# Input norm on a transposed copy of the input, by halves of the tokens, and group 0's values with 512 moving columns

## The chip, the cores and the metric

The kernel runs on one core of one Trainium2 chip. The metric is the device time of one execution in microseconds (us), from the first to the last instruction with the launch around them. The engines are TensorE (PE; its weight loads are PEld), VectorE (DVE), ScalarE (ACT), GpSimd (POOL) and SyncE (SP), which here only issues DMAs. The granted clock is the share of full speed that TensorE was given: 1.00 is 2.4 GHz, 0.50 is 1.2 GHz.

## The reference

One decoder block on 1024 tokens of width 1024, in float32: an RMS norm, one wide projection, an LRU mixer and a windowed attention mixer side by side, then a feed-forward part. The change concerns the first lines and the values `v` of attention group 0:

```python
def rms_norm(x, g):
    y = x * lax.rsqrt(jnp.mean(x * x, axis=-1, keepdims=True) + 1e-6)
    return y * g

h = rms_norm(x, pre_mix_norm)
proj = h @ w_in                       # (1024, 1024) @ (1024, 8704)
xr, gr, q, k, v, gates = jnp.split(proj, split_at, axis=-1)
v = v.reshape(B, S, 3, 4, 128)        # 3 groups of 4 heads of 128
```

Groups 1 and 2 take their keys and values at a stride of 4 and 16 tokens; group 0 takes them in order.

## The kernel before

**Precision.** Each float32 operand of a large product is split into a high part `hi` (float32r, one copy on ACT or POOL) and a low part `lo` (one subtraction on DVE or POOL). A product is three matmuls, hi hi, hi lo, lo hi, summed in PSUM (`mm3`, L128 to L133). Matmuls of two plain float32 operands are used for attention scores and values.

**The start.** `x` is loaded in 8 blocks of 128 tokens, tokens on the partitions (`load_x`). For a block, `norm_rows` squares and sums it on ACT (L192), works out the rate in five small operations (`rstd_of`, L176 to L185) and multiplies on DVE (L193). `turn` transposes it with 8 PE transposes (L201) and leaves three copies with channels on the partitions: `hth` (hi, L204), `htl` (lo, L205) and `hf` (full, L206), 2 tiles each of 4 x 128 channels by 1024 tokens. Ten matmuls on zeros (L153) run ahead. The main loop has eight turns of this; three of group 0's four `v_chain` steps stand in it (VAT), the fourth behind it.

**Group 0's values.** `v_weights(pr, 0)` loads and splits the weights of one pair of heads, 256 columns. `v_chain(pr, 0, wv, i)` multiplies 256 tokens, in two pieces of 128, by them: 48 matmuls with 256 moving columns, one copy from PSUM (L405), and after each second step a DMA to the DRAM tile `vd`. There are 4 steps for each of 2 pairs, 384 matmuls.

**Groups 2 and 1.** These use a two by two scheme of seven products instead of eight: tokens and channels are halved into blocks b11, b12, b21, b22, and `x_sums` forms t1 = b12 - b11, t2 = b22 - t1, t4 = b21 - t2, t3 = b22 - b12 on POOL (L457), in place in `hf` and in `x2`, and splits t1, t4, t3 at once (ACT L453, DVE L454). It stands in the loop over the second pair's four `v_chain` steps. t2 is split at L572 and L573 into the halves of `hth` and `htl` that held b12. Then `v_start(2)` does the two products that need only blocks of the input (96 matmuls), and `v_quad(2)` the other five: it loads four blocks of weights a21, a22, a11, a12 into `vr`, forms sums of them (`s3` at L551 on POOL, L552 and L553 on DVE, L554 on POOL), splits them and multiplies. `vr` and the other tiles of the pool `vq` lie in the memory of `hf` and `x2`, which is given back first. `decay_rates` is a chain of 14 DVE operations on 128 x 8 elements for the LRU part (L364 to L377).

**Order.** A tile scheduler orders each engine's queue; `issue_after` adds an edge. All loads of `load` go through SP's queue in the order in which the program has them.

## Time and profile before

| | us |
|---|---|
| median of 3 runs (1767.65 to 1770.36) | 1769.05 |
| the profiled execution, its own time | 1767.89 |
| its span, first to last instruction | 1766.0 |

| engine | busy us | share of the span |
|---|---|---|
| PE | 1683.0 | 95% |
| PEld | 1393.4 | 79% |
| DVE | 1154.1 | 65% |
| POOL | 770.6 | 44% |
| ACT | 753.6 | 43% |

The times of instructions count from the start of the span. What is said of sums refers to the profiled execution; the median is 1.16 above it. A time range of a stage is given with the busy time of every engine in it; an idle engine matters only where the next thing that ends the program waits for it.

### The profile page before, as it was taken

Reading aid. Unit: us, or ns where it says so; the run is one execution under the profiler, and the core shown is the slowest. Engines: PE = TensorE matmul, PEld = TensorE weight load, DVE = VectorE, ACT = ScalarE, POOL = GpSimd, SP = SyncE. Lnnn points to the kernel's source line nnn. Section 1 sums busy time; section 2 is a strip of 40 time slices with the busy share of each in tenths; the row PEclk is TensorE's granted clock in tenths of the full one; section 3 lists DMA queues with packets and bytes.
Section 4 is the critical chain, followed back from the end, with each engine's and each line's share of the span. In section 5 each row is a group of like instructions: output and inputs, shape, how many; then the busy total and the mean of one; then the engine's idle time right before and its main releaser. Section 6 shows DMA issues by size and latency. Waiting matters only on the chain.

```text
span 1766.0 us, 22080 instructions
## 1 busy us (share of the span) xinstructions
PE 1683.0 (95%) x7994; PEld 1393.4 (79%) x7994; DVE 1154.1 (65%) x1669; ACT 753.6 (43%) x1244; POOL 770.6 (44%) x698
## 2 busy tenths in 40 slices
PE   7799999999999998989999999799999999999897
PEld 6789888778787786778888887678888888788685
DVE  6667477687889855654343577855555465558958
ACT  6333356655455532365442244522232222354443
POOL 3433444456354554306233303577656656404503
PEclk8899999999999999999999999899999999999999
DMA  4244343334233366485526752133322222474363
GB/s 174 96 153 137 132 141 125 132 131 149 108 136 127 137 197 190 157 298 214 193 96 250 273 204 84 52 111 113 118 103 100 101 90 101 145 273 157 118 209 113
DMA packets 95437, 262.17 MB, mean 148 GB/s; under 512 B 14448, under 2 KB 22672, under 8 KB 93920
## 3 DMA queue, kind: packets, MB, share of 16 engines
q1 hardware_dynamic: 69504, 178.82, 29.7%
...
HBM read 177.52 MB, written 83.10 MB: 148 GB/s over the span
## 4 chain that ended last, share of the span: by engine, by line
PE 73%; DVE 12%; DMA 5%; issue 4%; POOL 3%; ACT 2%; SPq 1%; DVEq 0%; POOLq 0%; ACTq 0%
PE pq L133 14%; PE pq L132 14%; PE pq L131 14%; PE pd L1199 2%; PE py L133 2%; PE pd L1198 2%; PE pd L1200 2%; PE py L132 2%; PE py L131 2%; DMA rsn<-rtd 2%; PE pv L132 2%; PE pv L133 2%; PE pv L131 2%; PE po L883 2%; DVE wlo L97 1%
## 5 line engine op out<-in xcount | busy, mean ns | idle before, releaser
L133 PE MATMUL pq<-hth,wlo 128*128 128x512 f32 x448 | 177.9, 397 | 7.4 <-DVE wlo L97 7.4
L132 PE MATMUL pq<-htl,whi 128*128 128x512 f32 x448 | 179.8, 401 | 0.0
L131 PE MATMUL pq<-hth,whi 128*128 128x512 f32 x448 | 178.6, 399 | 0.0
L277 POOL TENSOR_TENSOR sb<-wraw 128x512 f32<-128x512 f32 x50 | 67.7, 1353 | 164.3 <-DMA wraw<-in_w_fg 89.2
L96 ACT ACTIVATE whi<-sa 128x1024 fp32r<-128x1024 f32 x50 | 52.9, 1059 | 202.1 <-PE pq L132 128.1
L1199 PE MATMUL pd<-fbl,fah 128*128 128x512 f32 x300 | 117.7, 392 | 7.9 <-DVE fbl L97 7.1
L97 DVE TENSOR_TENSOR wlo<-wraw,whi 128x1024 fp32r<-128x1024 f32 x69 | 105.8, 1533 | 23.9 <-ACT whi L96 21.1
L1200 PE MATMUL pd<-fbh,fal 128*128 128x512 f32 x300 | 116.8, 389 | 0.0
L1198 PE MATMUL pd<-fbh,fah 128*128 128x512 f32 x300 | 116.7, 389 | 0.0
L96 ACT ACTIVATE whi<-wraw 128x1024 fp32r<-128x1024 f32 x69 | 72.8, 1055 | 85.5 <-PE pq L132 31.7
L133 PEld LDWEIGHTS pq<-hth,wlo 128*128 128x128 f32 x448 | 85.2, 190 | 29.3 <-DVE wlo L97 8.8
L319 DVE TENSOR_TENSOR uw<-pq,uw 128x512 f32<-128x512 f32 x100 | 68.3, 683 | 54.8 <-PE pq L133 53.6
L131 PEld LDWEIGHTS pq<-hth,whi 128*128 128x128 f32 x448 | 85.1, 190 | 21.3
L132 PEld LDWEIGHTS pq<-htl,whi 128*128 128x128 f32 x448 | 85.2, 190 | 20.1
L97 DVE TENSOR_TENSOR fal<-ar,fah 128x512 fp32r<-128x512 f32 x75 | 66.9, 892 | 38.4 <-ACT fah L96 38.4
L1105 POOL TENSOR_TENSOR fo<-fo,ut 128x512 f32<-128x512 f32 x44 | 60.1, 1368 | 69.3 <-DVE ut L1104 69.3
L97 DVE TENSOR_TENSOR wlo<-sa,whi 128x1024 fp32r<-128x1024 f32 x50 | 69.7, 1395 | 30.0 <-ACT whi L96 29.9
L591 DVE TENSOR_TENSOR fb<-pq,uw 128x512 f32<-128x512 f32 x84 | 67.8, 808 | 28.6 <-PE pq L133 28.1
L132 PE MATMUL pv<-wlo,hth 128*128 128x256 f32 x256 | 76.1, 297 | 7.7 <-DVE wlo L97 7.7
L133 PE MATMUL pv<-whi,htl 128*128 128x256 f32 x256 | 76.1, 297 | 5.3 <-DVE htl L205 4.4
L132 PE MATMUL pq<-t1l,whi 128*128 128x512 f32 x200 | 78.9, 395 | 0.0
L131 PE MATMUL pq<-t1h,whi 128*128 128x512 f32 x200 | 78.9, 394 | 0.0
...
## 6 DMA issues: line engine op xcount, KB each, us to landing
...
qkd<-fb POOLq DMA_DIRECT2D x24, 512.0 KB, 3.4
qk<-qkd SPq DMA_DIRECT2D x24, 512.0 KB, 9.0
wraw<-in_w_fg SPq DMA_DIRECT2D x24, 512.0 KB, 3.3
wraw<-in_w_fu SPq DMA_DIRECT2D x24, 512.0 KB
...
```

The lines of the kernel that those rows point to most:

```text
L96: A.activation(hi, src, AF.Copy)
L97: (le or V).tensor_sub(lo, src, f(hi))
L131: T.matmul(o, lh, rh, start=(first and i == 0), stop=False)
L132: T.matmul(o, lh, rl, start=False, stop=False)
L133: T.matmul(o, ll, rh, start=False, stop=(last and i == n - 1))
L277: G.tensor_add(sb[:, lo_], r1[:, lo_], r1[:, hi_])
L319: V.tensor_add(y, bank, x)
L591: V.tensor_add(o, half_in(bank, g), half_in(add, g))
L1105: G.tensor_mul(g, g, ut)
L1198: T.matmul(o, ah[:, ts], bh, start=(i == 0), stop=False)
L1199: T.matmul(o, ah[:, ts], bl, start=False, stop=False)
L1200: T.matmul(o, al[:, ts], bh, start=False, stop=(i == NP - 1))
```

## The change

The host gives the kernel `xT`, the transposed input, and the weights of group 0 in four blocks of 256 channels by 512 columns (`w_v0`); `w_v` holds only groups 1 and 2 now. The input is loaded straight into `hf`, channels on the partitions, in eight pieces of 2 x 128 channels by 512 tokens. A sum over channels is then a sum over partitions: `sums` multiplies the squares with a column of ones (32 matmuls of one column for each half of the tokens), `rates` works out the four rates of a partition, writes them on the diagonals of four 128 x 128 blocks and multiplies with a matrix of ones, so that `prb` holds each token's rate on all partitions. `normed` multiplies `hf` by the gain and `prb` in place and splits it. `v0_mm` has tokens stationary and 512 weight columns moving. The constants come over ACT's queue. Two more groups of six matmuls on zeros are written (WARM2). The POOL subtractions of `x_sums` are now `x_diffs`, in two calls of 4 x 1024 columns within the second half; the splits of t1, t3 and t4 (`x_split`) are written behind `v_start(2)`, with `decay_rates` ahead of them.

```diff
-    def turn(xn, t, hi, lo, full):
...
-    for t in range(NT):
...
-        turn(xns[t], t, hth, htl, hf)
-        if t in VAT:
-            v_chain(0, 0, wv, VAT.index(t))
...
-    v_chain(0, 0, wv, 3)
+    def w0_split():
+        j = len(W0)
...
+        split(R0[j], hi, lo, he=G)
...
+    def squares(h, j):
+        SQ[h, j] = sp.tile([128, 2, 512], F32, name="sq", bufs=4)
+        A.activation(SQ[h, j], pair(hf, j, h), AF.Square)
+
+    def sums(h):
+        ss = ps("pss")
+        for j in range(4):
+            for k in range(2):
+                for t in range(4):
+                    T.matmul(ss[:, t:t + 1], SQ[h, j][:, k, 128 * t:128 * t + 128], ones[:, 0:1],
+                             start=(j + k + t == 0), stop=(j == 3 and k == 1), skip_group_check=True)
+        return ss[:, 0:4]
+
+    def rates(ss):
+        s = sp.tile([128, 4], F32, name="rs4", bufs=2)
+        last_act[0] = A.activation(s, ss, AF.Sqrt, bias=epsc, scale=1.0 / D)
...
+        for t in range(4):
+            V.tensor_scalar(dg[:, t], ident, e[:, t:t + 1], None, op0=OP.mult)
+        rb = ps("prb")
+        T.matmul(rb, ones, dg.rearrange("p t n -> p (t n)"), start=True, stop=True)
+        return rb
+
+    def normed(h, j, rb):
+        for k in range(2 * j, 2 * j + 2):
+            x = hf[k // 4][:, k % 4, 512 * h:512 * h + 512]
+            V.scalar_tensor_tensor(x, x, gneg[:, k:k + 1], rb, op0=OP.mult, op1=OP.mult)
+        x, hi = pair(hf, j, h), pair(hth, j, h)
+        last_act[0] = A.activation(hi, x, AF.Copy)
+        last_dve[0] = V.tensor_sub(pair(htl, j, h), x, f(hi))
+
+    def v0_mm(bk, h, j):
+        for k in range(2 * j, 2 * j + 2):
+            wh, wl = (t[:, k % 2] for t in W0[j])
+            for t in range(4):
+                c = slice(512 * h + 128 * t, 512 * h + 128 * t + 128)
+                T.matmul(bk[t], hTh[k][:, c], wh, start=(k == 0), stop=False)
+                T.matmul(bk[t], hTh[k][:, c], wl, start=False, stop=False)
+                T.matmul(bk[t], hTl[k][:, c], wh, start=False, stop=(k == KT - 1))
+
+    def v0_out(bk, h):
+        vs = sp.tile([128, 4, 512], F32, name="vs0", bufs=2)
+        for t in range(4):
+            A.activation(vs[:, t, :], bk[t], AF.Copy)
+        for pr in range(2):
+            G.dma_start(v_block(pr, 0, h), vs[:, :, 256 * pr:256 * pr + 256])
+
+    def x_diffs(j):
+        b11, b12, b21, b22 = (pair(hf, 2 * u + j, h) for u in range(2) for h in range(2))
+        x2p = x2[:, 2 * j:2 * j + 2, :]
+        G.tensor_sub(b11, b12, b11)
+        G.tensor_sub(x2p, b22, b11)
+        G.tensor_sub(b21, b21, x2p)
+        G.tensor_sub(b12, b22, b12)
+
+    for j in range(4):
+        x_load(0, j)
+        squares(0, j)
...
+    ss = sums(0)
+    keep_warm(WARM2)
+    rb = rates(ss)
+    keep_warm(WARM2)
+    bk = [ps("pv") for _ in range(4)]
+    for j in range(4):
+        normed(0, j, rb)
+        with tc.issue_after(last_act[0].ins):
+            squares(1, j)
+        if j == 3:
+            ss1 = sums(1)
+        v0_mm(bk, 0, j)
...
+    rb = rates(ss1)
+    normed(1, 0, rb)
+    with tc.issue_after(last_act[0].ins):
+        v0_out(bk, 0)
+    for j in range(1, 4):
+        normed(1, j, rb)
+    bk = [ps("pv") for _ in range(4)]
+    for j in range(4):
+        v0_mm(bk, 1, j)
+        if j in (1, 3):
+            x_diffs(j // 2)
+    v0_out(bk, 1)
...
-    wv = v_weights(1, 0)
-    for i in range(4):
-        v_chain(1, 0, wv, i)
-        x_sums(4 + i, hf, x2[:, :, 128 * i:128 * i + 128], X1, ("t1", "t3", "t4"))
...
     b = v_start(2)
-    for k in range(4):
-        A.activation(X1["t2"][0][:, k, :], x2[:, k, :], AF.Copy)
-        V.tensor_sub(X1["t2"][1][:, k, :], x2[:, k, :], f(X1["t2"][0][:, k, :]))
+    with tc.issue_after(last_act[0].ins), tc.issue_after(last_dve[0].ins):
+        x_split("t2", x2)
+        x_split("t1", hf[0][:, :, LO])
+        x_split("t3", hf[0][:, :, HI])
+        x_split("t4", hf[1][:, :, LO])
```

On PE the program now starts with these rows (`pw` are the matmuls on zeros, `pss` the sums of squares, `prb` the broadcast rates, `pv` group 0):

```order
L156 MATMUL pw<-wz 128x512 x11
L426 MATMUL pss<-ones,sq 128x1 x8
L156 MATMUL pw<-wz 128x512 x6
L426 MATMUL pss<-ones,sq 128x1 x8
L156 MATMUL pw<-wz 128x512 x5
L426 MATMUL pss<-ones,sq 128x1 x16
L444 MATMUL prb<-dg,ones 128x512
L460 MATMUL pv<-whi,hth_110 128x512
```

The matmuls on zeros of both later calls stand among the sums, and none behind them.

On DVE, in the kernel before, these rows stand in the stretch of group 0's second pass (`lv` is the decay chain, t1l to t4l are the low parts of the sums for groups 2 and 1):

```order
L373 SCALAR_TENSOR_TENSOR lv<-lv 128x8 x6
L374 SCALAR_TENSOR_TENSOR lv<-lv 128x8
L375 SCALAR_TENSOR_TENSOR lv<-lv 128x8
L454 TENSOR_TENSOR t1l_617<-hf_111,t1h_616 128x4x128
L376 TENSOR_SCALAR lv<-lv 128x8
L454 TENSOR_TENSOR t4l_621<-hf_112,t4h_620 128x4x128
L377 TENSOR_SCALAR lv<-lv 128x8
L454 TENSOR_TENSOR t3l_619<-hf_111,t3h_618 128x4x128
```

After the change they stand behind t2 and behind the second weight split of `v_start(2)`, directly ahead of `v_quad(2)` (L619 writes its first outputs, L635 and L636 are its sums of weights):

```order
L529 TENSOR_TENSOR htl_112<-x_116,hth_110 128x2x512
L361 SCALAR_TENSOR_TENSOR lv<-lv 128x8
L98 TENSOR_TENSOR wlo<-wraw,whi 128x1024
L361 SCALAR_TENSOR_TENSOR lv<-lv 128x8 x4
L362 SCALAR_TENSOR_TENSOR lv<-lv 128x8
L363 SCALAR_TENSOR_TENSOR lv<-lv 128x8
L529 TENSOR_TENSOR t1l_552<-hf_114,t1h_551 128x1024 x2
L529 TENSOR_TENSOR t3l_554<-hf_114,t3h_553 128x1024 x2
L529 TENSOR_TENSOR t4l_556<-hf_115,t4h_555 128x1024 x2
L619 TENSOR_TENSOR vs<-pv,vp_689 128x512 x2
L635 TENSOR_TENSOR vr<-vr 128x1024
L636 TENSOR_TENSOR vr<-vr 128x1024
```

The six splits have moved from the loop to the end of it, and read whole tiles of `hf` (hf_114 and hf_115 here) in whose memory `vr` lies.

On POOL the eight subtractions now stand between the issue of the first half's outputs and that of the second's (x_116 is `x2`, vs_394 and vs_521 the two halves of the outputs):

```order
L475 TENSOR_TENSOR hf_114<-hf_114 128x2x512 x2
L469 DMA vd<-vs_394 512x1x256 x2
L476 TENSOR_TENSOR x_116<-hf_115,hf_114 128x1024
L478 TENSOR_TENSOR hf_114<-hf_115,hf_114 128x2x512
L477 TENSOR_TENSOR hf_115<-hf_115,x_116 128x2x512
L476 TENSOR_TENSOR x_116<-hf_115,hf_114 128x1024
L478 TENSOR_TENSOR hf_114<-hf_115,hf_114 128x2x512
L477 TENSOR_TENSOR hf_115<-hf_115,x_116 128x2x512
L469 DMA vd<-vs_521 512x1x256 x2
```

Before, they were 16 of half the size, four to each `v_chain` step of the second pass.

## Rows read from the trace of the kernel before

**Rows 1.** The page: the span, PE's busy time, and the chain that ended last by engine.

```profile
span 1766.0 us, 22080 instructions
PE 1683.0 (95%) x7994; PEld 1393.4 (79%) x7994; DVE 1154.1 (65%) x1669; ACT 753.6 (43%) x1244; POOL 770.6 (44%) x698
PE 73%; DVE 12%; DMA 5%; issue 4%; POOL 3%; ACT 2%; SPq 1%; DVEq 0%; POOLq 0%; ACTq 0%
```

**Rows 2.** Busy time of each engine by stage: from and to, the length, then busy us with the count of instructions for each engine, the granted clock, the share of the DMA engines and GB/s.

```profile
0.00:19.80 19.80, 7.75 (x26) 6.17 (x27) 10.80 (x22) 8.05 (x16) 8.16 (x10) 0.73 0.73 280
19.80:100.80 81.00, 69.09 (x530) 68.06 (x528) 53.69 (x86) 39.28 (x75) 27.54 (x21) 0.90 0.29 101
100.80:105.70 4.90, 1.05 (x5) 0.63 (x5) 4.86 (x6) 3.06 (x3) 3.09 (x2) 0.88 0.18 64
```

**Rows 3.** PE in order of time, the start: start us, duration us, engine, line, operation, out<-in, shape, count, and in brackets the idle time before and what ended it.

```profile
2.02 4.19 PE L153 MATMUL pw<-wz 128*128 128x512 f32 x10 [2.02 <-DVE wz L150]
...
19.82 0.56 PE L131 MATMUL pv<-whi,hth 128*128 128x256 f32 x1
...
26.84 1.91 PE L201 MATMUL pT<-cst,xn 128*128 128x128 f32 x16
```

**Rows 4.** PE in order of time, the end of `v_start(2)` and the beginning of `v_quad(2)`, same columns.

```profile
99.77 0.28 PE L133 MATMUL pv<-whi,htl 128*128 128x256 f32 x1
...
100.48 0.28 PE L133 MATMUL pv<-whi,htl 128*128 128x256 f32 x1
102.23 0.51 PE L131 MATMUL pv<-whi,hth 128*128 128x256 f32 x2 [1.47 <-ACT whi L96]
...
105.67 0.58 PE L132 MATMUL pv<-wlo,hth 128*128 128x256 f32 x1 [1.99 <-DVE wlo L97]
```

**Rows 5.** The other engines in order of time ahead of 105.67, same columns.

```profile
98.61 1.21 DVE L552 TENSOR_TENSOR vr<-vr 128x1024 f32<-128x1024 f32 x1
99.86 1.22 DVE L553 TENSOR_TENSOR vr<-vr 128x1024 f32<-128x1024 f32 x1
...
101.60 2.21 DVE L481 CAST ang<-pos_i 128x512 f32<-128x512 int32 x1
...
104.41 2.34 DVE L97 TENSOR_TENSOR wlo<-vr,whi 128x1024 fp32r<-128x1024 f32 x2
...
101.12 2.00 ACT L96 ACTIVATE whi<-vr 128x1024 fp32r<-128x1024 f32 x2 [5.42 <-DVE vr L553]
...
101.17 2.37 POOL L554 TENSOR_TENSOR vr<-vr 128x1024 f32<-128x1024 f32 x1 [7.48 <-DVE vr L553]
```

**Rows 6.** SP's queue in order of time (the row with a start), and the DMA view of 64 to 84 us: issues by destination and source with their count, KB each and the median us from issue to landing.

```profile
70.66 1.75 SPq L107 DMA_DIRECT2D vr<-in_w_v  x4
...
vr<-in_w_v SPq DMA_DIRECT2D x4, 512.0 KB, 6.9
...
vd<-vs POOLq DMA_DIRECT2D x1, 512.0 KB, 2.9
```

**Rows 7.** DVE and POOL in order of time within the subtractions for groups 2 and 1, same columns as rows 3.

```profile
59.85 0.68 DVE L454 TENSOR_TENSOR t1l<-hf,t1h 128x512 fp32r<-128x512 f32 x1
59.86 1.81 POOL L457 TENSOR_TENSOR hf<-hf,hf 128x512 f32<-128x512 f32 x1
60.46 1.25 DVE L376 TENSOR_SCALAR lv<-lv 128x8 f32<-128x8 f32 x1
61.62 0.68 DVE L454 TENSOR_TENSOR t4l<-hf,t4h 128x512 fp32r<-128x512 f32 x1
61.64 1.78 POOL L457 TENSOR_TENSOR hf<-hf,x 128x512 f32<-128x512 f32 x1
62.22 1.23 DVE L377 TENSOR_SCALAR lv<-lv 128x8 f32<-128x8 f32 x1
```

**Rows 8.** PE later in the program: two matmuls of 512 columns, six apart; all rows of L767, a float32 matmul of attention scores (duration ns least, median and longest, first and last start); and two weight loads that stand close together.

```profile
186.45 0.40 PE L131 MATMUL pq<-hth,whi 128*128 128x512 f32 x1
...
187.85 0.40 PE L131 MATMUL pq<-hth,whi 128*128 128x512 f32 x1
...
L767 PEld LDWEIGHTS psc<-qk x104: 186/192/333, 758.0 to 908.2; 128*128 128x128 f32 x104
...
805.45 0.13 PEld L829 LDWEIGHTS ptr<-cst,rwc 8*128 8x128 f32 x1 [0.37 <-DVE st L783]
805.60 0.20 PEld L871 LDWEIGHTS ppt<-cst,pb 128*128 128x128 f32 x2
```

**Rows 9.** The DMA view of 0 to 12 us: GB/s in 40 equal slices of 0.3 us.

```profile
GB/s 0 0 0 0 0 55 259 96 109 205 341 355 410 437 369 382 273 219 369 424 369 424 424 410 335 335 410 396 423 437 437 410 423 437 437 410 423 423 369 410
```

**Rows 10.** Groups of instructions from 0 to 106 us: busy us, mean ns of one, and idle time before.

```profile
L96 ACT ACTIVATE whi<-vr 128x1024 fp32r<-128x1024 f32 x3 | 3.1, 1052 | 5.9 <-DVE vr L553 5.4 <-POOL vr L554 0.4
...
L551 POOL TENSOR_TENSOR vs<-vr 128x1024 f32<-128x1024 f32 x1 | 2.4, 2419 | 0.0
...
L97 DVE TENSOR_TENSOR wlo<-vr,whi 128x1024 fp32r<-128x1024 f32 x2 | 2.3, 1208 | 0.0
...
L536 DVE TENSOR_TENSOR vs<-pv,vp 128x512 f32<-128x512 f32 x2 | 1.4, 688 | 6.7 <-issue 6.7
...
L183 DVE TENSOR_SCALAR rq<-rq 128x1 f32<-128x1 f32 x8 | 1.2, 154 | 0.3
```

**Rows 11.** Busy time by stage, same columns as rows 2, after the idle time before 105.67.

```profile
106.00:108.00 2.00, 2.00 (x11) 2.00 (x11) 2.00 (x3) 0.00 (x0) 0.00 (x0) 0.50 0.78 231
108.00:110.00 2.00, 2.00 (x11) 2.00 (x11) 0.55 (x2) 0.00 (x0) 0.00 (x0) 0.50 0.93 295
110.00:112.00 2.00, 2.00 (x14) 2.00 (x14) 1.02 (x2) 0.00 (x0) 0.00 (x0) 0.66 0.81 291
```

More of the change, by code (lines that the diff above doesn't have):

```diff
@@ L29 @@
 WARM = 10
+WARM2 = 6
 PRE = 4
@@ L148, in block, with keep_warm @@
     A.activation(warm, warm, AF.Sqrt)
-    wz = b4("wz", F32R)
+    epsc = sp.tile([128, 1], F32, name="epsc")
+    V.memset(epsc, EPS)
+    gneg = sp.tile([128, 8], F32, name="gneg")
+    wz = sp.tile([128, 640], F32R, name="wz")
     V.memset(f(wz), 0.0)
+    ones = sp.tile([128, 128], F32, name="ones")
+    V.memset(ones, 1.0)
     pw = ps("pw")
-    for i in range(WARM):
-        T.matmul(pw, wz[:, 0:128], wz[:, 128:640], start=True, stop=True)
-    xs = [load_x(0)]
-    gpre = gain_bc(a["g_pre"], "gpre", A)
+    def keep_warm(n):
+        for i in range(n):
+            T.matmul(pw, wz[:, 0:128], wz[:, 128:640], start=True, stop=True)
+    keep_warm(WARM)
     cst = const.tile([128, C_END], F32, name="cst")
-    c_ld = G.dma_start(cst, a["consts"])
-    vec = const.tile([128, 64], F32, name="vec")
+    A.dma_start(cst, a["consts"])
+    vec = const.tile([128, V_GP], F32, name="vec")
+    A.dma_start(gneg, a["vecs"][:, V_GP:V_END])
+    A.dma_start(vec, a["vecs"][:, 0:V_GP])
     ident = cst[:, C_ID:C_ID + 128]
@@ L167, in block @@
     last_dve = [None]
-    @contextmanager
-    def later():
-        with tc.issue_after(last_act[0].ins), tc.issue_after(last_dve[0].ins):
-            yield
     def rstd_of(ss):
@@ L194, in norm_rows @@
         return xn
-    def turn(xn, t, hi, lo, full):
-        for u in range(2):
-            p = ps("pT")
-            for j in range(4):
-                kt = 4 * u + j
-                T.transpose(p[:, 128 * j:128 * j + 128], xn[:, 128 * kt:128 * kt + 128], ident)
-            c = slice(128 * t, 128 * t + 128)
-            pv = p.rearrange("p (k n) -> p k n", k=4)
-            A.activation(hi[u][:, :, c], pv, AF.Copy)
-            V.tensor_sub(lo[u][:, :, c], pv, f(hi[u][:, :, c]))
-            A.activation(full[u][:, :, c], pv, AF.Copy)
     def nat(t, g):
@@ L430, in block, with pair, x_load, w0_load @@
-    with later():
+    LO, HI = slice(0, 512), slice(512, 1024)
+    def pair(ts, j, h):
+        return ts[j // 2][:, 2 * (j % 2):2 * (j % 2) + 2, 512 * h:512 * h + 512]
+    def x_load(h, j):
+        load(pair(hf, j, h), a["xT"][256 * j:256 * j + 256, 512 * h:512 * h + 512].rearrange("(k p) n -> p k n", p=128))
+    W0, R0 = [], []
+    def w0_load():
+        j = len(R0)
+        R0.append(wraw() if j < 2 else sp.tile([128, 1024], F32, name="w0r", bufs=2))
+        load(R0[j], a["w_v0"][j])
@@ new lines, in block @@
+    for j in range(4):
+        x_load(0, j)
+        squares(0, j)
+    for step, arg in (("w", 0), ("w", 1), ("x", 0), ("x", 1), ("w", 2), ("x", 2), ("x", 3), ("w", 3)):
+        w0_load() if step == "w" else x_load(1, arg)
+    V.tensor_scalar(gneg, gneg, -0.5, None, op0=OP.mult)
+    w0_split()
+    ss = sums(0)
[10 more added lines that the diff above has]
+        v0_mm(bk, 0, j)
+        if j < 3:
+            with tc.issue_after(last_dve[0].ins):
+                w0_split()
@@ L441, in block, with x_split @@
     X1["b22"] = hth[1][:, :, HI], htl[1][:, :, HI]
+    def x_split(n, src):
+        for j in range(2):
+            c = slice(2 * j, 2 * j + 2)
+            A.activation(X1[n][0][:, c], src[:, c], AF.Copy)
+            V.tensor_sub(X1[n][1][:, c], src[:, c], f(X1[n][0][:, c]))
     def x_sums(t, fl, x2c, X, names):
@@ L525, in v_start @@
     def v_start(g):
-        return [v_mm(wunit(a["w_v"][0, g, u]), n) for u, n in enumerate(("b11", "b21"))]
+        return [v_mm(wunit(a["w_v"][0, g - 1, u]), n) for u, n in enumerate(("b11", "b21"))]
     def v_quad(g, b, nxt, eng):
@@ L548, in v_quad @@
         for n in (2, 3, 0, 1):
-            load(r[n], a["w_v"][n // 2, g, n % 2])
+            load(r[n], a["w_v"][n // 2, g - 1, n % 2])
         s3 = raw("vs3")
```

65 lines of the change are left out of this document (26 added, 39 removed).

## Prediction, written before the changed kernel was run

> **What bounds the kernel now.** I read the page first: PE is busy for 95% of the span and holds 73% of the chain that ended last [rows 1]. A change can therefore pay only where PE waits or runs at half clock, and this one touches nothing behind the first 106 us. Next I read the busy time by stage [rows 2]. Up to 19.8 us PE is busy for only 7.8 us; from 19.8 to 100.8 it is busy for 69.1 of 81.0 us; from 100.8 to 105.7 for 1.1 of 4.9. Then the order of time of PE, DVE, ACT, POOL and SP in those stages. The reader is to see three things.
>
> First, group 0 begins at 19.82 [rows 3]. The last of the 480 matmuls of group 0 and of `v_start(2)` starts at 100.48, and the first quad of group 2 (`v_quad(2)`) runs steadily only from 105.67 [rows 4]. With the last 96 of them at 0.118 us each, group 0 itself ends at about 89.5. **105.67 is the time against which everything below is measured**, because from there on both programs issue the same work.
>
> Second, what holds PE until 105.67 is not group 0 but a chain on the other engines: two DVE sums from 98.61, two ACT copies from 101.12, a POOL subtraction from 101.17, a DVE cast, and the split from 104.41 [rows 5]. Their inputs, the four `vr` loads, were issued from 70.66 on and needed 6.9 us to land [rows 6]: 20 us early, and so invisible.
>
> Third, DVE and POOL take turns. At 59.85 a DVE subtraction runs 0.68 us; POOL's, started with it, takes 1.81 instead of its 1.25; the next DVE instruction, 8 columns wide, takes 1.25 because it waits for POOL's end; and again at 61.62 [rows 7]. With two operands in SBUF, each of the two waits out the other's whole instruction.
>
> **The change part by part.**
>
> *The 512 columns.* 384 matmuls of 256 columns become 192 of 512. Six steps of the first kind take 0.71 us (99.77 to 100.48) [rows 4], so 0.118 each and 45.4 us in all; six of the second take 1.40 us [rows 8], so 0.233 each and 44.8 us. The gain is 0.6 us. Leaving out 64 transposes saves 64 times 0.119 (16 in 1.91 us [rows 3]) = 7.6 us.
>
> *The start.* Ahead of the last quarter of the first half of `xT` come 2.4 MB (2.1 of x, 0.3 of constants). The old start moved as much by 8.9 us [rows 9], so I let it land at 9.5, and its square ends at 10.6. PE's queue is later than that: 11 warm matmuls at half clock (ten took 4.19 us [rows 3]) end at 6.5, then come 64 weight loads with one column each and 11 more warm ones. Why 64: an fp32 matmul that the code writes once stands twice in the trace (L767: 52 written, 104 recorded [rows 8]), and `sums` writes 32. No row shows a one-column matmul. Bounds for a pass: 0.06, the step between two loads at 805.60 (0.20 less 0.14 for the second itself) [rows 8]; 0.119, a transposed block of 128 columns [rows 3]. Nearer the first in columns, nearer the second in being part of a long run: I take 0.085. So 6.5 + 64 x 0.085 + 11 x 0.233 = 14.7.
>
> The Trainium skill (TensorE: Matmul & The Clock Gate, section on LDWEIGHTS) makes a weight load as long as its columns over 1.2 GHz, an estimate of 0.107 us here. By it the sum below would end 2.5 us later; the 0.06 step in the trace disagrees with it.
>
> From 14.7: a square root and four small DVE operations (0.15 to 0.2 each), four diagonal blocks (0.9), one weight split ahead of the last two (1.2) with one POOL conversion before it (0.6), the fp32 broadcast `prb` at half clock (1.9), two multiplications at 0.6 and a copy at 1.0 [rows 10]: 8.2 us. Group 0 begins at **22.9**, 3.1 later than before.
>
> *Half 0.* 96 matmuls at 0.233 = 22.4; a cold start, as at 106 to 110 (granted clock 0.50, that is 1.2 GHz, after the idle time before 105.67 [rows 11]), costs 2.1; the second half's sums stand in the middle with 64 x 0.085 = 5.4: 53.0. `prb` for the second half stands behind the last of them, 0.9: **53.9**. The splits on DVE and ACT are ahead here.
>
> *Half 1 and what moved into it.* PE waits 2.3 for the first block (two multiplications and a copy), 1.8 more for its `htl`, which POOL holds up, and needs 22.4 for the matmuls: group 0 ends at 80.4, `v_start(2)`, 96 times 0.118, at 91.8. So on PE alone the change wins 9 us. But the whole of `x_diffs` (8 POOL subtractions of 1024 columns, 2.35 each [rows 10]) now begins at 56.2, when before most of it and all `t1`, `t3`, `t4` splits lay under the second pass of group 0. Turn by turn with the DVE splits, weight splits and decay operations that stand between them, it ends at 82.3: 18.8 of POOL's own, 5.9 for the DVE instructions that get a turn and for late inputs, 1.4 for issuing two DMAs. DVE, which got one instruction per POOL instruction, then still has 14 decay operations (2.8 us) and two splits (2.3), with the steps between them to 87.6; only then the six splits `t1`, `t3`, `t4`, 1.15 each: **94.5**. (ACT's side of `t4` waits for the write of `vs0`, issued by 83.8 and, with the 2.9 us of [rows 6], landed by 87; that is in time.)
>
> *The load that loses its cover.* `vr` lies where `hf` was. SP issues the second of the four loads only when the last split of `t4` has read `hf[1]`, and POOL's `s3` needs the third. Before, this cost nothing, under group 0's second pass; now it lies bare. From 94.5: two issues and two loads, 5.4 (bounds 3 for one load alone and the 6.9 of [rows 6]), to 99.9; POOL's `s3` 2.4, to 102.3; two DVE sums, to 104.7; copy, cast, POOL's turn, two small ones and the split, 5.1 where the old stretch from 101.08 to 105.67 took 4.6 [rows 5]: **109.8**. PE idles 18 us before it and starts at half clock, as it does at 105.67 now, so that costs nothing new.
>
> *The rest* (constants on ACT's queue, `gneg`, W0's loads, the 1 KB pieces of `vs0`) hides under the first 20 us or under `v_start(2)`; uncovered, a write would cost its landing, 2.9 us.
>
> **Sum.** 109.8 - 105.7 = +4.1 us on the profiled execution, 1767.89, which is 1772.0; the median of the runs is 1.2 above that execution, so **1773**. About 0.2% (3.5 us) is what a measurement of this kernel tells from no change.
>
> **The rivals.**
>
> *1. It is faster, because DVE and POOL overlap in the second half.* Place: the eight subtractions on 3-dimensional blocks. If DVE's turns cost nothing, the splits end at 88.5 rather than 94.5 and DVE's cast isn't held: PE resumes at 101.5, or at 98.3 with a pass of 0.06. That is -4 to -7, about 1763 in the median. It decides from the moment at which `t4`'s last split ends before 90.3. For it: PE really gains 9 us, and a pass of 0.06 alone brings 90.7. Against it: the turns of [rows 7] show no exception for operands in SBUF.
>
> *2. The one-column passes cost more, and it is clearly slower.* If PE's clock falls to 1.2 GHz during a run of them, each doubles and the work behind starts cold, twice: 116.2, or 119.1 with the upper pass; a pass of 0.19, the full length of a 128-column load among the L767 rows [rows 8], gives 122.6. So +10 to +17, about 1781. For it: no row shows what the clock does in such a run. Against it: the transposes ran at full clock after 22 us. The Trainium skill (FP8 and Floating Point Precision, TensorE Precision Notes) gives true fp32 four passes, which would lead here; the trace records two.
>
> *3. It does nothing measurable.* The 9 us won on PE are given back almost exactly: a pass of 0.06 ends the sum at 106.0, +0.3, about 1769.5.
>
> **How the numbers follow.** The forecast with passes of 0.07 to 0.119 and a load of 4.5 to 6.5 us, +1.5 to +8, holds 0.50; rival 1 holds 0.20, rival 2 holds 0.15, rival 3 holds 0.15. Of the forecast, 0.15 lies under +3.5. So faster 0.20 (all of rival 1), same 0.30, slower 0.50. Its own range is 1770 to 1777. The 8-in-10 range reaches into rival 1 to -7 and into rival 2 to +15 on the median: 1762 to 1784.
>
> **What would show it.** After: first `pv` matmul near 23; `prb` for the second half near 54; last `t4l` near 94; `vr`'s third load landing near 100; a PE gap of 15 to 20 us between `v_start(2)` and `v_quad(2)`, ended by a DVE split near 110, and the same stages behind it as now. Wrong would be: no such gap (the load isn't what is waited for), `pss` passes outside 0.06 to 0.12, or POOL's subtractions at 2.35 with DVE busy beside them.

## The result, and the profile after

The changed kernel takes 1790.95 us, the median of 4 runs (1785.41 to 1796.57); the kernel before, beside it, 1768.56. The ratio is 1.0119, with a 95% interval of 1.0100 to 1.0137. The prediction was slower, 1773, with a range that ended at 1784: the sign was right, the size was not, and the time lies outside the range.

The profiled execution took 1796.57 us. The page of it, the same lines as [rows 1]: span, busy time, chain by engine.

```profile
span 1794.8 us, 21765 instructions
PE 1707.7 (95%) x7882; PEld 1404.1 (78%) x7882; DVE 1154.0 (64%) x1642; ACT 741.4 (41%) x1196; POOL 768.1 (43%) x688
PE 73%; DVE 12%; issue 5%; DMA 5%; POOL 3%; ACT 2%; SPq 1%; DVEq 0%; ACTq 0%; POOLq 0%
```

PE has 112 matmul records fewer than before and is busy 24.7 us longer. Of these, 19.1 stand ahead of the steady `v_quad(2)` (96.9 us of busy time there, against 77.9 in [rows 2]). Here is PE in order of time at the start (start us, duration, engine, line, operation, out<-in, shape, count; in brackets the idle time before and what ended it), without the matmuls of group 0 but its first.

```profile
1.65 4.71 PE L156 MATMUL pw<-wz 128*128 128x512 f32 x11 [1.65 <-DVE wz L149]
7.48 2.04 PE L426 MATMUL pss<-ones,sq 128*128 128x1 f32 x16 [1.12 <-ACT sq L418]
9.38 2.91 PE L156 MATMUL pw<-wz 128*128 128x512 f32 x6
12.09 2.09 PE L426 MATMUL pss<-ones,sq 128*128 128x1 f32 x16
14.04 1.41 PE L156 MATMUL pw<-wz 128*128 128x512 f32 x5
15.29 6.14 PE L426 MATMUL pss<-ones,sq 128*128 128x1 f32 x32
24.72 2.08 PE L444 MATMUL prb<-dg,ones 128*128 128x512 f32 x2 [3.29 <-DVE dg L442]
29.48 0.77 PE L460 MATMUL pv<-whi,hth 128*128 128x512 f32 x1 [2.68 <-ACT hth L452]
...
48.05 11.72 PE L426 MATMUL pss<-ones,sq 128*128 128x1 f32 x64
67.22 1.02 PE L444 MATMUL prb<-dg,ones 128*128 128x512 f32 x2
```

The 64 passes of the second half take 11.72 us, 0.18 each; 16 of the first half take 2.09, 0.13 each with the last one's own length in it. The same instruction has two prices. The busy time by stage shows why (from and to, length, then busy us with counts for PE, its loads, DVE, ACT, POOL, the granted clock, DMA share, GB/s).

```profile
14.00:16.00 2.00, 2.00 (x15) 1.78 (x14) 0.00 (x0) 0.00 (x0) 0.27 (x1) 1.00 1.04 398
16.00:18.00 2.00, 2.00 (x12) 2.00 (x11) 0.00 (x0) 0.00 (x0) 0.78 (x1) 0.51 1.05 390
...
48.00:50.00 2.00, 2.00 (x20) 1.96 (x19) 0.00 (x0) 0.00 (x0) 0.00 (x0) 1.00 0.00 0
50.00:52.00 2.00, 2.00 (x13) 2.00 (x12) 0.00 (x0) 0.00 (x0) 0.00 (x0) 0.54 0.00 0
52.00:54.00 2.00, 2.00 (x11) 2.00 (x11) 0.00 (x0) 0.00 (x0) 0.00 (x0) 0.50 0.00 0
...
62.00:64.00 2.00, 2.00 (x7) 1.57 (x6) 0.00 (x0) 0.00 (x0) 0.00 (x0) 0.55 0.00 0
64.00:66.00 2.00, 2.00 (x10) 1.64 (x9) 0.00 (x0) 0.00 (x0) 0.00 (x0) 1.00 0.00 0
```

At 50 us PE has not been idle for 20 us, and is recorded as busy for 2.00 of 2.00 us; yet the granted clock falls from 1.00 to 0.50 (2.4 to 1.2 GHz) within the run of one-column passes, and comes back at 64, 4 us after matmuls of 512 columns have begun again. From the start of one pass to the next it is 0.112 us at 1.00 and 0.213 at 0.50.

Behind the second `prb` everything came as worked out, only later. DVE, SP, POOL and PE in order of time, the rows that answer to [rows 4 to 6]:

```profile
68.28 2.72 DVE L450 SCALAR_TENSOR_TENSOR hf<-hf,gneg,prb 128x512 f32<-128x512 f32 x4 [6.41 <-PE prb L444]
...
105.86 2.35 DVE L529 TENSOR_TENSOR t4l<-hf,t4h 128x1024 fp32r<-128x1024 f32 x2
...
105.97 3.55 SPq L108 DMA_DIRECT2D vr<-in_w_v  x4
...
114.06 2.34 POOL L634 TENSOR_TENSOR vs<-vr 128x1024 f32<-128x1024 f32 x1 [3.55 <-DMA vr<-in_w_v]
...
117.69 1.23 DVE L636 TENSOR_TENSOR vr<-vr 128x1024 f32<-128x1024 f32 x1
...
120.06 0.80 PE L132 MATMUL pv<-whi,hth 128*128 128x256 f32 x2 [12.20 <-ACT whi L97]
...
122.13 2.35 DVE L98 TENSOR_TENSOR wlo<-vr,whi 128x1024 fp32r<-128x1024 f32 x2
...
123.40 0.58 PE L133 MATMUL pv<-wlo,hth 128*128 128x256 f32 x1 [1.60 <-DVE wlo L98]
```

| us | predicted | profile after |
|---|---|---|
| sums of the first half end | 14.7 | 21.4 |
| first `pv` matmul | 22.9 | 29.5 |
| second `prb` ends | 53.9 | 68.2 |
| last `t4l` ends | 94.5 | 108.2 |
| POOL's `s3` begins (third `vr` load) | 99.9 | 114.1 |
| `v_quad(2)` runs steadily | 109.8 | 123.4 |

From the second `prb` to `v_quad(2)` the prediction has 55.9 us, the profile 55.2. So 17.7 of the loss stand at 123.4 against 105.67. The other 11.1 come behind it, where both programs issue the same work in the same order.

### The profile page after: what moved, and what is told of

Same layout as the page of the kernel before. It is cut to its first block, busy times and chain, and to the rows that moved or that the text cites. A ratio compares the mean times of both kernels' runs of the same rounds, so it can differ in the third digit from the quotient of the medians.

```text
span 1794.8 us, 21765 instructions
## 1 busy us (share of the span) xinstructions
PE 1707.7 (95%) x7882; PEld 1404.1 (78%) x7882; DVE 1154.0 (64%) x1642; ACT 741.4 (41%) x1196; POOL 768.1 (43%) x688
## 3 DMA queue, kind: packets, MB, share of 16 engines
q0 software_dynamic: 21024, 78.96, 11.7%
q8 instruction: 62, 1.02, 0.2%
## 4 chain that ended last, share of the span: by engine, by line
PE 73%; DVE 12%; issue 5%; DMA 5%; POOL 3%; ACT 2%; SPq 1%; DVEq 0%; ACTq 0%; POOLq 0%
PE pq L134 15%; PE pq L133 15%; PE pq L132 15%; PE pd L1284 2%; PE pd L1285 2%; PE pd L1283 2%; PE py L134 2%; PE py L133 2%; PE py L132 2%; PE po L968 2%; PE pv L133 1%; PE pv L134 1%; PE pv L132 1%; PE pss L426 1%; DVE fal L98 1%
## 5 line engine op out<-in xcount | busy, mean ns | idle before, releaser
L265 POOL TENSOR_TENSOR sb<-wraw 128x512 f32<-128x512 f32 x50 | 71.3, 1425 | 173.1 <-DMA wraw<-in_w_fg 92.0
L98 DVE TENSOR_TENSOR wlo<-wraw,whi 128x1024 fp32r<-128x1024 f32 x69 | 106.4, 1542 | 28.7 <-ACT whi L97 26.2
L1285 PE MATMUL pd<-fbh,fal 128*128 128x512 f32 x300 | 116.8, 389 | 0.0
L307 DVE TENSOR_TENSOR uw<-pq,uw 128x512 f32<-128x512 f32 x100 | 68.4, 684 | 52.8 <-PE pq L134 51.4
L98 DVE TENSOR_TENSOR wlo<-sa,whi 128x1024 fp32r<-128x1024 f32 x50 | 70.1, 1403 | 33.3 <-ACT whi L97 33.3
L266 POOL TENSOR_TENSOR sa<-sb,wraw 128x512 f32<-128x512 f32 x50 | 78.9, 1578 | 0.0
L134 PE MATMUL pq<-t1h,wlo 128*128 128x512 f32 x200 | 78.6, 393 | 0.0
```

The lines of the kernel that those rows point to most:

```text
L98: (le or V).tensor_sub(lo, src, f(hi))
L134: T.matmul(o, ll, rh, start=False, stop=(last and i == n - 1))
L265: G.tensor_add(sb[:, lo_], r1[:, lo_], r1[:, hi_])
L266: G.tensor_sub(sa[:, lo_], sb[:, lo_], r0[:, lo_])
L307: V.tensor_add(y, bank, x)
L1285: T.matmul(o, al[:, ts], bh, start=False, stop=(i == NP - 1))
```

## The experiments

Twelve kernels ran. The table holds what their profiles show; "rest" is the span less the start of the steady `v_quad(2)`.

| kernel | first `pv` | second `prb` ends | `v_quad(2)` | from `prb` | rest | median us | ratio to before, 95% |
|---|---|---|---|---|---|---|---|
| before, first profile | 19.8 | | 105.7 | | 1660.3 | 1769.05 | |
| before_again | 19.7 | | 104.7 | | 1667.1 | 1773.66 (one run) | |
| after, first profile | 29.5 | 68.2 | 123.4 | 55.2 | 1671.4 | 1790.95 | 1.0100 to 1.0137 |
| after_again | 33.5 | 73.0 | 128.0 | 55.0 | 1662.2 | 1790.11 | 1.0084 to 1.0137 |
| e1_wide | 20.6 | 51.3 | 106.4 | 55.0 | 1669.5 | 1775.18 | 0.9994 to 1.0032 |
| e2_early | 33.0 | 61.8 | 116.8 | 55.1 | 1663.8 | 1789.10 | 1.0060 to 1.0147 |
| e3_dvediff | 33.6 | 73.0 | 123.9 | 51.0 | 1672.1 | 1790.41 | 1.0074 to 1.0141 |
| e4_ratesearly | 23.5 | 33.3 | 95.8 | 62.5 | 1663.7 | 1761.37 | 0.9919 to 0.9960 |
| e5_all | 23.5 | 33.3 | 95.8 | 62.5 | 1663.5 | 1761.66 | 0.9918 to 0.9954 |
| e6_loads | 31.6 | 71.1 | 126.9 | 55.8 | 1667.7 | 1790.47 | 1.0074 to 1.0117 |
| e7_nowarm2 | 29.0 | 68.6 | 123.6 | 55.0 | 1665.3 | 1790.69 (one run) | |
| e8_outlate | 23.4 | 33.2 | 94.9 | 61.7 | 1668.4 | 1762.03 | 0.9918 to 0.9964 |
| e9_cols256 | 20.8 | 53.3 | 107.7 | 54.4 | 1661.3 | 1773.86 | 0.9987 to 1.0027 |
| e10_s3first | 23.7 | 33.4 | 93.5 | 60.1 | 1667.4 | 1760.84 | 0.9913 to 0.9949 |

The kernel before had medians of 1768.56 to 1773.62 beside these, and single runs from 1766.66 to 1778.51. So the ratios are to be compared, each against the runs beside it, not the medians of two rows.

### The changed kernel once more

No edit.

> The changed kernel once more, unchanged. In its first profile v_quad(2) runs steadily from 123.4 us, 17.7 later than before (105.67), but the program ends 28.8 later: 11 us more are lost behind 123.4, in small pieces at many places, though both programs issue the same work there in the same order. Theory 1 (what is lost behind v_quad(2) differs from execution to execution): the start repeats within 0.5 us (first pv matmul 29.5, second prb ends 68.2, v_quad(2) 123.4), and the rest, 1671.4 us from there to the end in the first profile against 1660.3 before, comes out somewhere else between 1660 and 1672. Theory 2 (the change itself slows the later stages): the rest is 1671 again within 1 us.

Neither theory in full. The rest is 1662.2, so the 11 us are not the change's (theory 1). But the start does not repeat: the first `pv` matmul comes at 33.5, 4 us later, since more of the first half's passes ran at half clock.

```profile
7.49 3.01 PE L426 MATMUL pss<-ones,sq 128*128 128x1 f32 x16 [1.62 <-ACT sq L418]
10.36 2.91 PE L156 MATMUL pw<-wz 128*128 128x512 f32 x6
13.06 3.41 PE L426 MATMUL pss<-ones,sq 128*128 128x1 f32 x16
```

The same 16 passes take 3.01 and 3.41 us where they took 2.04 and 2.09. From the second `prb` on the stretch is 55.0 again.

### The sums with 128 columns of ones

```diff
-                    T.matmul(ss[:, t:t + 1], SQ[h, j][:, k, 128 * t:128 * t + 128], ones[:, 0:1],
+                    T.matmul(ss[:, 128 * t:128 * t + 128], SQ[h, j][:, k, 128 * t:128 * t + 128], ones,
...
-        return ss[:, 0:4]
+        return ss.rearrange("p (t n) -> p t n", n=128)[:, :, 0]
```

> The sums of squares multiply with 128 columns of ones instead of one; nothing else differs. Theory A (the clock falls because these passes move one column each, and it is the clock that mis-sized my sum): a pass stays at 0.11 us, the granted clock at 1.00 through both runs of sums, the first pv matmul comes at about 26 instead of 29.5, the second prb ends at about 58 instead of 68.2, and as all behind it is the same chain of 55 us, v_quad(2) at about 113 instead of 123.4: 10 us less, about 1781. Theory B (long runs of float32 weight loads lower the clock, whatever they move): passes of 0.21 again, v_quad(2) within 1 us of 123.4, 1791. Theory C (128 float32 columns cost more than the load): passes of more than 0.15 at full clock, v_quad(2) between 113 and 123.

PE's two runs of sums:

```profile
7.24 7.41 PE L426 MATMUL pss<-ones,sq 128*128 128x128 f32 x64 [1.19 <-ACT sq L418]
...
37.55 7.31 PE L426 MATMUL pss<-ones,sq 128*128 128x128 f32 x64
```

Two stages inside them, with the columns of the stages above:

```profile
10.00:12.00 2.00, 2.00 (x20) 2.00 (x19) 0.00 (x0) 1.19 (x2) 0.22 (x1) 1.00 1.01 401
...
40.00:42.00 2.00, 2.00 (x20) 2.00 (x19) 0.00 (x0) 0.00 (x0) 0.00 (x0) 1.00 0.00 0
```

128 times the output columns, and 7.3 us instead of 11.7: the clock stays at 1.00 and a pass steps at 0.112, as with one column at full clock. Theories B and C fall. The gain is larger than theory A said, 17 us at `v_quad(2)` and not 10: 8.0 in half 0 (20.61 to 51.33 is 30.7 us, where the changed kernel took 38.8), 6.8 at the end of the first sums (14.65, against 21.43: the scheduler now put the eleven later warm matmuls behind the sums, nine of them ahead of the first `prb`, which I had not counted), and 2.1 between there and the first `pv` (the broadcast at full clock, one weight split earlier). The second run of sums stands where it stood, between the same matmuls, so there the columns are all that differs. The time, 1775.18, is that of the kernel before within the interval.

### Squares and sums of the second half early

```diff
     rb = rates(ss)
     keep_warm(WARM2)
+    for j in range(4):
+        squares(1, j)
+    ss1 = sums(1)
...
-        with tc.issue_after(last_act[0].ins):
-            squares(1, j)
-        if j == 3:
-            ss1 = sums(1)
```

> The squares and sums of the second half stand right behind those of the first, ahead of most of group 0, still with one column each (five square tiles instead of four). Theory A (what counts is when the second half's rates are known, since 55 us of DVE, POOL and load work hang on them): the second prb ends at about 44 instead of 68.2, the last t4l at 84 to 88 instead of 108.2, and v_quad(2) is then held by PE's own work, at 100 to 105 instead of 123.4: about 1770. Theory B (the sums cost what they cost on PE, wherever they stand): group 0 begins about 11 us later (40), v_quad(2) 2 to 4 us earlier than 123.4, about 1788.

Neither, because the edit moved too little. The sums were done at 42.3 and the rates on DVE at 48.7, but `prb` stood where it had stood in PE's queue, behind half 0, and DVE waited for it:

```profile
61.78 2.72 DVE L450 SCALAR_TENSOR_TENSOR hf<-hf,gneg,prb 128x512 f32<-128x512 f32 x4 [13.07 <-PE prb L444]
```

`v_quad(2)` follows 55.1 us after that `prb`, as in the others: it is the broadcast that starts the chain, not the sums. It came 6.6 us earlier than in the first profile of the changed kernel; in the time, 1789.10 against 1790.11, nothing is to be seen. Of the moved passes 32 ran at half clock (6.83 us) and 32 at full clock, in two runs of 16 with matmuls of 512 columns around them; the second run, at 40.43, took the same time as the first:

```profile
37.01 1.84 PE L426 MATMUL pss<-ones,sq 128*128 128x1 f32 x16
```

### Rates and broadcast early too, with wide sums

```diff
     for j in range(4):
         normed(0, j, rb)
+        if j == 1:
+            rb1 = rates(ss1)
...
-    rb = rates(ss1)
+    rb = rb1
     normed(1, 0, rb)
```

This on top of the two edits above.

> 128 columns of ones in the sums, and for the second half not only squares and sums but also the rates and their broadcast ahead of most of group 0 (the experiment with early sums alone had left the second prb behind half 0 in PE's queue, where DVE waited 13 us for it). In five profiles v_quad(2) came 51 to 55 us after the second prb, whatever went before. Theory A (what hangs on the second half's rates is a fixed chain on DVE, POOL and the vr loads; started earlier it lies under group 0 until something else is later): DVE begins the second half at about 33 instead of 51.3, but t4's high part must wait for the write of the second half's outputs, some 10 us behind the end of group 0 at 70; the last t4l ends at about 80 instead of 91.3, v_quad(2) comes at 92 to 97 instead of 106.4: about 10 us less than with wide sums alone, 1765. Theory B (the sums and rates in the way of group 0's beginning cost what they save): v_quad(2) within 2 us of 106.4, about 1775.

Theory A holds: 95.8. The second `prb` ends at 33.3, PE does 260 matmuls from 32.74 to 83.00 without a wait, and the chain of 55 us is 62.5 long, because it now waits for group 0's outputs. DVE, ACT and SP in order of time:

```profile
73.34 2.36 DVE L530 TENSOR_TENSOR t1l<-hf,t1h 128x1024 fp32r<-128x1024 f32 x2 [7.64 <-ACT t1h L529]
...
77.78 2.01 ACT L529 ACTIVATE t4h<-hf 128x1024 fp32r<-128x1024 f32 x2 [1.63 <-DMA vd<-vs]
...
78.01 4.54 SPq L108 DMA_DIRECT2D vr<-in_w_v  x4
```

The ratio is 0.9939: this version beats both kernels.

### The subtractions on DVE

```diff
-        G.tensor_sub(b11, b12, b11)
-        G.tensor_sub(x2p, b22, b11)
-        G.tensor_sub(b21, b21, x2p)
-        G.tensor_sub(b12, b22, b12)
+        V.tensor_sub(b11, b12, b11)
+        V.tensor_sub(x2p, b22, b11)
+        V.tensor_sub(b21, b21, x2p)
+        V.tensor_sub(b12, b22, b12)
```

> The eight subtractions of x_diffs on DVE (1.2 us each) instead of POOL (2.4 to 2.9 each and turn by turn with DVE, 25.3 us from the first to the last). Theory A (the turns of DVE and POOL set the end of the splits): DVE has 34.5 us of its own work from 68.3, the last t4l ends at 103 instead of 108.2, v_quad(2) at 118 instead of 123.4, about 1786. Theory B (t4's high part waits on ACT for the write of the second half's outputs, to 102.55 in the first profile, whatever DVE does): the last t4l ends at 105.8, v_quad(2) at 121, about 1788.5. Theory C (POOL's subtractions cost nothing here): no change, 123.4.

The absolute times I gave are off, as the second `prb` came at 73.0 in this execution; after_again, with the same 73.0, is the one to compare. `v_quad(2)` comes 4.0 earlier than there, between theories A and B. In the changed kernel two splits of DVE among POOL's subtractions took 10.21 us:

```profile
75.17 10.21 DVE L453 TENSOR_TENSOR htl<-hf,hth 128x1024 fp32r<-128x1024 f32 x2
```

Here no DVE instruction of this size takes over 1.23, the subtractions included, and the last `t4l` is then held by the write of the outputs, as theory B had it:

```profile
86.26 1.22 DVE L476 TENSOR_TENSOR x<-hf,hf 128x1024 f32<-128x1024 f32 x1
...
105.93 2.01 ACT L528 ACTIVATE t4h<-hf 128x1024 fp32r<-128x1024 f32 x2 [1.65 <-DMA vd<-vs]
```

The Trainium skill (SBUF — State Buffer, section "Who interferes with whom") gives DVE and GpSimd an exclusive lock on a shared pair of ports when a DVE instruction has two inputs in SBUF and the other one reads it. These rows and [rows 7] agree. In the time, 4 us are not to be seen against a spread of 14 between single runs.

### The order of the vr loads

```diff
-        for n in (2, 3, 0, 1):
+        for n in (2, 0, 1, 3):
             load(r[n], a["w_v"][n // 2, g - 1, n % 2])
```

> The changed kernel with the four vr loads in the order a21, a11, a12, a22; nothing else differs. Theory A (the vr loads lie bare behind t4's last split and are on the path): POOL's vs3 begins before the last t4l ends, the first DVE sum about 4 us after that split instead of 8.2, and v_quad(2) about 51 us after the second prb instead of 55. Theory B (the loads are not waited for): 55 us as before. The time itself moves with the clock at the start, so 1786 to 1791 either way; the stretch from the second prb to v_quad(2) decides.

Theory B by the number, 55.8, though not for its reason. POOL's subtraction does begin earlier, 4.3 us behind the last `t4l` instead of 5.8, but not before its end, as SP's first load itself waits for `t3l` (108.84 here). The first DVE sum then waits for the load that is now last:

```profile
115.39 2.33 POOL L634 TENSOR_TENSOR vs<-vr 128x1024 f32<-128x1024 f32 x1 [2.02 <-DMA vr<-in_w_v]
...
119.62 1.23 DVE L635 TENSOR_TENSOR vr<-vr 128x1024 f32<-128x1024 f32 x1 [7.34 <-DMA vr<-in_w_v]
```

All four loads lie bare; which of them is last only decides who waits. What they would cost if they lay elsewhere was not tried.

### Without the later warm matmuls

```diff
-WARM2 = 6
+WARM2 = 0
```

> The changed kernel without the eleven warm matmuls of the two later calls. Theory A (these matmuls don't hold the clock, as the profiles show it falling through the one-column passes with them in place; they only stand in the queue): the clock falls as before, the first sums follow the squares at 0.21 a pass, so that they end at about 15 to 18 instead of 21.4 to 25.4, the first pv matmul comes at 23 to 26 instead of 29.5 to 33.5, v_quad(2) at 117 to 121. Theory B (they keep the clock up in the first half of the sums): passes at 0.21 from the first one on and a later or equal end, 21 to 25.

Mostly theory B, and I had it wrong: here the clock does not fall in the first passes, it had not risen yet. That goes by the step of the passes, 0.213, which is their price at 0.50 in the changed kernel; the granted clock reads 1.00 beside it. PE in order of time, and a stage inside the passes:

```profile
1.65 4.63 PE L156 MATMUL pw<-wz 128*128 128x512 f32 x10 [1.65 <-DVE wz L149]
7.15 13.81 PE L426 MATMUL pss<-ones,sq 128*128 128x1 f32 x64 [0.87 <-ACT sq L418]
...
10.00:12.00 2.00, 2.00 (x11) 2.00 (x10) 0.00 (x0) 1.09 (x2) 0.32 (x1) 1.00 1.01 398
```

The 64 passes take 0.216 each, with the last one's own length in it. They end at 20.96, which is no later than with the eleven matmuls (21.4 and 25.4): what these bought in clock they cost in time, in the one execution that there is.

### Wide sums, with 256 columns

```diff
-                T.matmul(bk[t], hTh[k][:, c], wh, start=(k == 0), stop=False)
+                for n in (LO2, HI2):
+                    T.matmul(bk[t][:, n], hTh[k][:, c], wh[:, n], start=(k == 0 and n is LO2), stop=False, skip_group_check=True)
...
```

> The kernel with wide sums, but group 0's values in matmuls of 256 columns again (768 instead of 192 and of the old 384: tokens and channel blocks stay as they are, so each weight load of 128 tokens serves two matmuls of 256 columns). By the steps in the trace of before (0.118 a matmul of 256 columns, 0.233 of 512) group 0 gets 0.3 us longer in either half: v_quad(2) within 0.5 us of 106.4 and the same time, 1775. If the steps of 256 columns are longer here, at most by the old ones at half clock (0.213), it is visible in the 72 rows ahead of the second sums: 17.1 us in the kernel with wide sums.

(The count in it is a slip: it is 384 matmuls, as many as before, and each has a weight load of its own.) Two stages of this kernel, and then the second of them in the kernel with wide sums:

```profile
20.00:24.00 4.00, 3.20 (x15) 3.23 (x16) 4.00 (x5) 3.49 (x4) 1.73 (x1) 0.59 0.30 116
28.00:32.00 4.00, 4.00 (x37) 4.00 (x36) 4.00 (x5) 3.52 (x4) 0.00 (x0) 1.00 0.00 0
```

```profile
28.00:32.00 4.00, 4.00 (x19) 3.22 (x18) 4.00 (x5) 3.33 (x4) 0.00 (x0) 1.00 0.00 0
```

From 28 to 32 us there are 37 matmuls instead of 19 of 512 columns: about twice as many of half the size, as by [rows 4, 8]. Half 0 is 32.5 us long instead of 30.7, more than the 0.3 expected; its first 4 us ran at a granted clock of 0.59, where the kernel with wide sums had 1.00. Whether the smaller matmuls brought that about was not tried. The second `prb` ends 2.0 later, `v_quad(2)` comes 1.4 later, and the time is the same within the interval, 1773.86. In the time the 512 columns buy no more than the prediction gave them, within what can be told.

### The three ways to go on from the early rates

e5_all: early rates, subtractions on DVE, loads in the other order.

> Wide sums, early rates, the subtractions of x_diffs on DVE, and the four vr loads in the order a21, a11, a12, a22, so that only the last of them lies where t4 is read. If each part has its own price (subtractions on DVE 4 us, measured; the third load no longer waiting for t4's last split, 4 us by the 8.2 us between that split and the first sum of weights): the last t4l at about 80, v_quad(2) at 88 to 92, 14 to 17 us before the 105.7 of the kernel before: 1752 to 1758. If the write of the outputs or v_start(2) on PE is then what is waited for, v_quad(2) stays at 93 to 97 and the time at about 1760.

The second case, to the number: 95.8, as without the two additions. DVE waits for ACT in any case: 7.64 us ahead of `t1l` in e4_ratesearly, 9.56 here.

e8_outlate: early rates, and group 0's last outputs written behind the splits, through tiles `vs` of the pool `vp`.

```diff
-        vs = sp.tile([128, 4, 512], F32, name="vs0", bufs=2)
...
+            vs = vp.tile([128, 4, 256], F32, name="vs")
...
-    v0_out(bk, 1)
...
+    with tc.issue_after(last_act[0].ins):
+        v0_out(bk, 1)
```

> Wide sums and early rates, and besides the second half's outputs of group 0 are copied and written behind the splits of t1, t3 and t4, through tiles whose memory these splits don't reuse. With early rates alone, ACT idled 1.6 us for the write of these outputs and 2.7 for their copies ahead of t1's split (72.26), DVE 7.6, the first vr load was issued at 78.0, when t3's last split had ended, and v_quad(2) came at 95.8. Theory A (the loads behind the splits are still what is waited for, and they follow the splits): t3's last split ends at about 73, the loads are issued then, v_quad(2) comes at 90 to 92, 1756 to 1758. Theory B (v_start(2), which ends at 83, or the copies now in the way of v_quad(2) hold it): 94 to 96, 1761.

Theory B by the number. The splits end 3.9 earlier (`t4l` at 77.4), `v_quad(2)` only 0.9, at 94.9. Two new waits took the place of the old one:

```profile
83.20 1.29 DVE L619 TENSOR_TENSOR vs<-pv,vp 128x512 f32<-128x512 f32 x2 [5.83 <-DMA vd<-vs]
...
84.78 0.78 POOL L625 DMA_DIRECT2D vd<-vs  x1 [6.22 <-DVE vs L619]
85.58 2.35 POOL L634 TENSOR_TENSOR vs<-vr 128x1024 f32<-128x1024 f32 x1
```

DVE waits for a tile that is still being written, and POOL, in order, holds its subtraction behind the issue of DVE's result.

e10_s3first: tiles of their own, and that issue behind the subtraction.

```diff
-            vs = vp.tile([128, 4, 256], F32, name="vs")
+            vs = vp.tile([128, 4, 256], F32, name="vs0")
...
-        G.tensor_sub(s3, a11, a21)
+        s3i = G.tensor_sub(s3, a11, a21)
...
-            G.dma_start(vd[pr, g, 512 * u:512 * u + 512].rearrange("(q p) n -> p q n", p=128), t)
+            with tc.issue_after(s3i.ins):
+                G.dma_start(vd[pr, g, 512 * u:512 * u + 512].rearrange("(q p) n -> p q n", p=128), t)
```

> The kernel with wide sums, early rates and late outputs, with two things more: the four output tiles of group 0 have buffers of their own (in the run before, v_quad(2)'s first output on DVE had waited for one of them until 83.2), and POOL's subtraction s3 stands ahead of the issue of that output's write (which had held s3 until 85.6, though its loads had landed earlier). Theory A (these two were the new waits): s3 begins at 77 to 79, the first DVE sum at about 84.5, when the two output sums behind the end of v_start(2) at 83 are done, and v_quad(2) comes 7 us later at 91 to 92 instead of 94.9; about 1758. Theory B (the loads themselves are as late): s3 not before 83, v_quad(2) at 94 to 95, 1762.

Nearer theory B: 93.5. Both waits are gone, and the loads are what is left: issued from 74.34, the third is there 9.8 us later.

```profile
84.14 2.33 POOL L635 TENSOR_TENSOR vs<-vr 128x1024 f32<-128x1024 f32 x1 [7.24 <-DMA vr<-in_w_v]
```

The four versions with early rates lie at 0.9931 to 0.9941, their intervals over one another; e4_ratesearly is the smallest edit of them.

### The kernel before once more

> The kernel before once more, unchanged. Theory 1 (the stretch behind the first steady v_quad(2) differs from execution to execution in any of these kernels; eleven profiles of the changed kernel and its variants show it between 1661.3 and 1672.1 us): the start repeats, v_quad(2) at 105.7 within 0.3, and the rest is somewhere between 1660 and 1672, most likely above the 1660.3 of its first profile. Theory 2 (before has a shorter rest than the changed kernel): 1660 to 1661 again.

Theory 1: the rest is 1667.1. The start is 1.0 earlier than in the first profile, where I allowed 0.3. In fourteen profiles the rest lies between 1660.3 and 1672.1, the two of the kernel before among them. The largest single piece stands in the attention stage, at the same matmuls in both kernels. PE in the first profile of before:

```profile
807.00 1.10 PE L883 MATMUL po<-pts,vt 128*128 128x128 f32 x8
```

In its second profile:

```profile
810.15 2.08 PE L883 MATMUL po<-pts,vt 128*128 128x128 f32 x8 [2.74 <-ACT pts L873]
```

In the changed kernel:

```profile
831.30 1.64 PE L968 MATMUL po<-pts,vt 128*128 128x128 f32 x8 [2.73 <-ACT pts L958]
```

In the first, PE goes on at once; in the other two it waits 2.7 us for ACT, and then works at half clock for a while (a granted clock of 0.90 over the 17 us around it, against 1.00 in the first). Unchanged code falls either way. What tips it was not tried.

## Why the prediction was wrong

**What bounds the kernel.** Right: `v_quad(2)` is held by the chain of splits, loads and sums, PE stands still for 15.5 us ahead of it but for four early matmuls (18 predicted), and the stages behind issue the same work.

**The price of a pass: the step that failed.** "64 x 0.085" stands in the sum twice, as if the clock were given. 0.112 at full clock is inside the bounds I gave and near the upper one; the row of [rows 3] that I called nearer by length was the right one, and the 0.06 of [rows 8], the step between two loads, was no price of a stream. The Trainium skill (TensorE: Matmul & The Clock Gate, section on LDWEIGHTS) had the better price, 0.107 by its rule, which I set aside for that row; the 0.112 at full clock agrees with it, the 0.213 at half clock does not, so here its one rate for a load fits full clock only.

But what mis-sized the sum most is the clock: counted by their starts, 72 of the 128 passes stepped at 0.213. The first sums end at 21.4 instead of 14.7, +6.7: the passes took 10.0 us instead of 5.4, the warm matmuls among them 4.0 instead of 2.6, and PE waited for the first squares until 7.48, where I had it begin at 6.5. (My sums fit a pass of 0.088 to 0.09 rather than the 0.085 stated: with that, 14.7 and 53.0 would be 14.5 and 52.8, and a pass of 0.06 would end the sum at 106.6, not 106.0.) Half 0 takes 38.8 instead of 31.0, +7.8: 11.6 instead of 5.4 for the sums, 7.6 instead of 5.6 for the 24 matmuls behind them, which start cold; the rest went 0.4 the other way.

With 128 columns the clock holds, and both ends lie near the predicted ones, first sums 14.65 (14.7), half 0 30.7 (31.0). That is luck, as the terms are others: each run of passes takes 7.1 to 7.2 us instead of 5.4 and the first one begins 0.7 later, but the eleven warm matmuls (2.6) stand behind the sums and the cold start of half 0 (2.1) does not come.

**Rival 2 was the case that happened, priced too low.** It named the clock's fall in such a run, with a chance of 0.15, and gave 119.1 with the upper pass and 122.6 with one of 0.19. It came to 123.4 and, in the second profile, 128.0. Its own words give more than its sum: 128 passes at twice 0.085 are 10.9 us more, 120.7 before any second cold start, and 116.2 does not come out of them. I also held the two records of a plain float32 matmul against it. But a record is not one pass of plain length: the two of the second `prb` take 1.02 us at full clock, the last alone 0.59, so 0.43 from one to the next, where a split matmul of as many columns steps at 0.233 [rows 8]. I held the transposes of before against it, which ran at full clock; but these move 128 columns each, and that is where the two differ.

**The start behind the sums.** From there to the first `pv` 8.05 us, predicted 8.2, though the terms that I listed add up to 7.8 at most.

**Half 1, turns, the load's lost cover.** Right to 1 us over 55: `x_diffs` took 25.3 us (26.1 predicted), POOL's `s3` began 5.8 behind the last `t4l` (5.4). The turns were real: without them 4.0 us less. That rival 1 needs them to vanish was the right reason against it.

**The 9 us that PE wins.** They are there. In the kernel with wide sums, where the clock holds, PE has done group 0 and `v_start(2)` at 92.3 (this row's start less its idle time), where before it was 100.8; predicted was 91.8:

```profile
103.03 0.80 PE L132 MATMUL pv<-whi,hth 128*128 128x256 f32 x2 [10.70 <-ACT whi L97]
```

With rates early as well it is 83.0, as PE then has no waits in half 1. The 9 us could not show while DVE, POOL and the loads ended later.

**The sum against the median.** I took the stages behind `v_quad(2)` as fixed, since the runs of before lay within 2.7 us. They differ by 12 from profile to profile. Of the 28.8 us between the two first profiles 17.7 are the change's and 11.1 the execution's. And the changed kernel's own start varies by 4.5 with the clock: `v_quad(2)` comes 17.7 and 22.3 later in its two profiles, and the medians are 22.4 apart. Both belong in a range; mine had neither.
